# Down projections of the channel mixers by Strassen's method, with the combined weights summed in DRAM

## The chip, the cores and the metric

The kernel runs on one core of a Trainium2 chip. The metric is the device time of one execution in microseconds (us). The time before is 1413.56 us, the median of three runs (1411.99 to 1413.66). A core has five engines, each with its own queue of instructions, worked off in order: PE (matrix products, with PEld loading its weights), DVE (elementwise work), ACT (activations and copies), POOL (a second, slower elementwise engine) and SP (which issues most transfers). Transfers run on 16 DMA engines that all queues share. DRAM is the chip's large memory.

## The reference

A trunk of two layers over 512 tokens of width 1024, in float32. Each layer has a token mixer (layer 0: retention and neighbourhood attention; layer 1: a state space mixer) and a channel mixer, both between norms:

```python
def conv_geglu_ffn(hn, w_up, conv_w, conv_b, w_down):
    u = depthwise_conv_centered(hn @ w_up, conv_w, conv_b)
    gate, val = jnp.split(u, 2, axis=-1)
    return (jax.nn.gelu(gate, approximate=True) * val) @ w_down

def reference(x, ...):
    for layer in range(DEPTH):
        ...
        x = x + rms_norm(m, norm_mix_post[layer])
        f = conv_geglu_ffn(rms_norm(x, norm_ffn_pre[layer]), ffn_w_up[layer], ffn_conv_w[layer],
                           ffn_conv_b[layer], ffn_w_down[layer])
        x = x + rms_norm(f, norm_ffn_post[layer])
    return x
```

The down projection takes a 512 x 2816 activation and a 2816 x 1024 weight to 512 x 1024.

## The kernel before

Every large product is made of three: an operand is split into a high part that PE takes without loss and the low rest (`split`, L92: ACT casts the high part, DVE subtracts to get the low one), and `mm3` (L102) adds high x high, low x high and high x low into one bank of PSUM. A weight tile is 128 x 1024 in float32, 512 KB: SP loads it into one of three buffers `wst` (`wload`, L61), and it is split into `whi` and `wlo`, four buffers each (`wunit`, L69).

The program runs mixer0, the channel mixer of layer 0, mixer1, the channel mixer of layer 1. In mixer0 the values are projected first; then four pairs of heads follow. For each pair `project` (L423 on) makes `rq` and `rk` with rotary: ACT copies the product to `ra`, SP moves its halves crosswise into `rb`, POOL multiplies `rb` by the sines (L444), DVE adds. So POOL has two `rb` for each pair. Ahead of the pairs POOL fills a tile `zero` (L414), and ACT copies it into four tiles (L419).

In the channel mixer (`ffn`, L237) an up projection makes 22 blocks of 128 channels; `tail` (L255) ends each with a convolution, the gate and a split into `hh` and `hl`. The down projection (`down_tm`, L208) then goes by output half n, weight tile and block of 128 tokens t: 22 blocks of channels x 4 blocks of tokens x 2 halves x 3 products, each of 512 columns. When a result (t, n) is complete, `post_half` (L167) takes its sum of squares on ACT and multiplies it by the norm's gains on DVE; `post_norm` adds it to x, `norm` makes the next norm, `turn` transposes it for the next stage.

The order of instructions on each engine is set at build time by a scheduler, which moves an instruction ahead as soon as its inputs are there by the scheduler's own reckoning; on the chip each engine then keeps to that order, and an instruction that waits holds all behind it on its engine. The listings below show that order.

Of the kernel before, what the change touches and what calls it, by code (L numbers as in the profile page):

```python
# [1 line left out]

# [5 lines left out]
F32 = mybir.dt.float32  # L8
# [13 lines left out]
EPS = 1e-6  # L22
FFN = 2816
NF = FFN // P


class Env:


    def __init__(self, ctx, tc):  # L30
        self.tc, self.nc = tc, tc.nc
        nc = self.nc
        pool = lambda name, bufs, **kw: ctx.enter_context(tc.tile_pool(name=name, bufs=bufs, **kw))
# [23 lines left out]
        self.xh = self.res.tile([P, KD, S], R32, name="xh")  # L57
        self.xl = self.res.tile([P, KD, S], R32, name="xl")
        self.late, self.xs, self.turned = [], {}, {}

    def wload(self, src, behind=None):  # L61

# [36 lines left out]
                self.together([m], [b])  # L99
        return first  # L100

    def mm3(self, out, lh, ll, rh, rl, first, last):  # L102
        mm = self.nc.tensor.matmul
        mm(out, lh, rh, start=first, stop=False)  # L104
        mm(out, ll, rh, start=False, stop=False)  # L105
        mm(out, lh, rl, start=False, stop=last)  # L106
# [60 lines left out]
    def post_half(self, st, t, n, ps, g_post, eng=None, m=None):  # L167
# [5 lines left out]
        halves = st.setdefault(t, [])  # L173
        r = self.inv_rms("m", halves[0][0], s) if halves else None
        (eng or nc.vector).tensor_tensor(m, ps, g_post[:, n * 512:(n + 1) * 512], op=ALU.mult)
        halves.append((s, m, r))

    def finish(self, steps, st, done, ahead=0):
        for step in steps.split():
# [13 lines left out]
    def post_norm(self, st, t):  # L193

        nc = self.nc
        (_, m0, _), (_, m1, r) = st[t]
        for h, m in enumerate((m0, m1)):
            xs = self.x[:, t, h * 512:(h + 1) * 512]
            nc.vector.scalar_tensor_tensor(xs, m, r, xs, op0=ALU.mult, op1=ALU.add)

# [33 lines left out]
    E.late += [lambda s=s: E.finish(s, st, done) for s in LATE]  # L234


def ffn(E, w_up, cw, w_down, g_post_row, done, w1=None):  # L237


    nc, tc = E.nc, E.tc  # L240
    with ExitStack() as ctx:
        hp = ctx.enter_context(tc.tile_pool(name="ffn_h", bufs=NF))
        cp = ctx.enter_context(tc.tile_pool(name="ffn_c", bufs=1))
        cwt = cp.tile([P, 2, NF, 4], F32, name="cwt")
        hs = []
# [18 lines left out]
        extra = lambda i=0: [hp.tile([P, S], R32, name=n) for n in ("hh", "hh", "hl", "hl")]  # L264
# [3 lines left out]
        w0 = [[u0, u1], [E.wunit(w_up[0, 1], extra(), st, behind=behind), E.wunit(w_up[1, 1], extra(), behind=behind)]]  # L268
        nc.sync.dma_start(cwt, cw)
        p0 = [[E.mm.tile([P, S], F32, name="mm") for s in range(2)] for f in range(2)]  # L270
        for c in range(2):
            for i in range(4):
                f, s = i // 2, i % 2
                E.proj_fm(p0[f][s], w0[f][s], c * 256, c * 256 + 256)
                if c == 0 and i in (1, 2):
                    E.flush()
        for f in range(2):
            tail(f, *p0[f])
        for f in range(2, NF):
            ps = []  # L280
# [6 lines left out]
            tail(f, *ps)  # L287
        g_post = E.bcast(g_post_row)
        batches = [[(0, u)] for u in (2, 2, 2, 2, 2, 1)] + [[(1, u)] for u in (2, 2, 1, 6)]
        down_tm(E, batches, w_down, lambda k: hs[k], g_post, done, lambda i: extra() if i not in (2, 3) else None)  # L290


def log1p_exp_neg(E, alloc, z):
# [35 lines left out]
def mixer0(E, w0, w_v, w_fm, tabs, dist_d, logit, gn, bias, w_out, g_post_row, done):  # L329
# [4 lines left out]
    with ExitStack() as ctx:  # L334
# [97 lines left out]

        def project(p, o, nm):
            i = ("rk", "rq", "rg", "nq", "nk").index(nm)
            w = E.wunit(w_fm[i, p])
            ps = E.mm.tile([P, S], F32, name="mm")
            E.proj_fm(ps, w)
            if i < 2:
                a = E.tmp.tile([P, S], F32, name="ra", tag="tmp")
                b = E.tmp.tile([P, S], F32, name="rb", tag="tmp")  # L440
                nc.scalar.activation(a, ps, AF.Copy, scale=1.0 if i else 0.125)
                for j in range(4):
                    nc.sync.dma_start(b[32 * j:32 * j + 32], a[32 * (j ^ 1):32 * (j ^ 1) + 32])
                nc.gpsimd.tensor_tensor(b, b, rot[:, 1], op=ALU.mult)  # L444
                nc.vector.tensor_tensor(a, a, rot[:, 0], op=ALU.mult)
# [561 lines left out]
def trunk(tc, x, norms, ab, ssd, ffns, out):  # L1007

    nc = tc.nc
    with ExitStack() as ctx:  # L1010
# [42 lines left out]
        ffn(E, *ffns[1], norms[1, 3], store, w1)  # L1053
        while E.late:
            E.flush()

# [8 lines left out]
def _rows(w, order=None):  # L1065

    k, n = w.shape
    w = w.reshape(k // P, P, n // 512, 512)
    if order is not None:
        w = w[list(order)]  # L1070
    return w.reshape(k // 256, 2, P, n // 512, 512).transpose(3, 0, 2, 1, 4).reshape(n // 512, k // 256, P, 1024)


def _rotary_tables(np):
# [23 lines left out]
def _layouts(np, i):  # L1098
# [34 lines left out]
    for l in range(2):  # L1133
        w = i["ffn_w_up"][l]
        a[f"f{l}_up"] = np.stack([_cols(w[:, s * FFN:(s + 1) * FFN]) for s in range(2)])
        cw = np.concatenate([i["ffn_conv_w"][l], i["ffn_conv_b"][l][None]])
        a[f"f{l}_cw"] = cw.reshape(4, 2, NF, P).transpose(3, 1, 2, 0)
        a[f"f{l}_down"] = _rows(i["ffn_w_down"][l])
    return {n: np.ascontiguousarray(v) for n, v in a.items()}


# [26 lines left out]
```

## Time and profile before

| | |
|---|---|
| median of three runs | 1413.56 us |
| span of the profiled execution, first to last instruction | 1409.7 us |
| PE's granted clock, mean | 0.999 |
| moved by DMA | 166.36 MB, mean 118 GB/s |
| DMA queues | SP's 150.00 MB (34.0% of 16 engines' span), ACT's 15.21 MB (3.8%), none of POOL |

The profile is one execution on the chip. An engine is busy while it executes; "idle before" names what ended its idle time. PE's products overlap, so their single durations add up to more than the time that they take together. The page gives no time of its own for the profiled execution; its span lies 3.9 us under the median of the runs.

### The profile page before, as it was taken

To read this page: it belongs to the slowest core of one execution; us is meant where nothing else is said; L and a number is where in the kernel's file an instruction comes from. 1 tells how busy PE (TensorE), PEld (TensorE's weight loads), DVE (VectorE), ACT (ScalarE), POOL (GpSimd) and SP (SyncE) were. 2 spreads that over 40 slices of the span, in tenths; PEclk is the share of its full clock that TensorE was granted. 3 is DMA by queue.
4 is the path that set the end of the run, shared out by engine and by line. 5 is a ranking of instruction groups with operands and counts; after the bars stand their busy time and mean duration, and the time that the engine had idled before them with its cause. 6 is when DMAs were issued, how large, how long until landed. Compare 5 with 4: busy or idle time off the path is not lost.

```text
span 1409.7 us, 18020 instructions
## 1 busy us (share of the span) xinstructions
PE 1386.0 (98%) x6908; PEld 1144.1 (81%) x6908; DVE 905.1 (64%) x1364; ACT 710.4 (50%) x1203; POOL 62.7 (4%) x66
## 2 busy tenths in 40 slices
PE   7999999999999999999999999999999999999998
PEld 6877787898888888888778787787888888888886
DVE  7378888755566652347878786897786565654232
ACT  5356665544444431324877787477454444442230
POOL 0010110100000000000000110010110000000000
PEclk9999999999999999999999999999999999999999
DMA  8443233222333233333566454273433333232231
GB/s 291 147 141 96 87 97 101 86 86 92 103 91 104 90 90 109 115 113 106 142 185 189 136 182 146 75 212 107 137 120 105 105 90 105 91 105 90 90 105 60
DMA packets 56438, 166.36 MB, mean 118 GB/s; under 512 B 6688, under 2 KB 7456, under 8 KB 56352
## 3 DMA queue, kind: packets, MB, share of 16 engines
q1 hardware_dynamic: 48464, 150.00, 34.0%
q10 hardware_dynamic: 7888, 15.21, 3.8%
q8 instruction: 55, 0.90, 0.3%
q14 instruction: 31, 0.25, 0.1%
HBM read 157.57 MB, written 5.51 MB: 116 GB/s over the span
## 4 chain that ended last, share of the span: by engine, by line
PE 88%; DVE 4%; ACT 3%; DMA 2%; issue 1%; POOL 1%; SPq 0%; DVEq 0%; POOLq 0%; ACTq 0%
PE mm L104 26%; PE mm L106 26%; PE mm L105 26%; PE pi L844 1%; PE st L793 1%; PE py L864 1%; PE pt L161 1%; PE pt L737 1%; PE y L519 1%; ACT pb L823 1%; DMA pb<-pd 0%; ACT junk L141 0%; DMA x<-in_x 0%; DVE wlo L96 0%; ACT whi L95 0%
## 5 line engine op out<-in xcount | busy, mean ns | idle before, releaser
L104 PE MATMUL mm<-xh,whi 128*128 128x512 f32 (+1 forms) x1216 | 463.9, 382 | 0.4 <-ACT xh L95 0.2
L105 PE MATMUL mm<-xh,wlo 128*128 128x512 f32 (+2 forms) x1216 | 462.8, 381 | 1.4 <-DVE wlo L96 1.4
L106 PE MATMUL mm<-xl,whi 128*128 128x512 f32 (+2 forms) x1216 | 463.2, 381 | 0.5 <-DVE xl L96 0.5
L96 DVE TENSOR_TENSOR wlo<-wst,whi 128x1024 fp32r<-128x1024 f32 (+1 forms) x208 | 254.3, 1224 | 137.3 <-ACT whi L95 135.6
L95 ACT CAST whi<-wst 128x1024 fp32r<-128x1024 f32 (+1 forms) x208 | 216.6, 1042 | 147.1 <-PE mm L105 117.7
L104 PEld LDWEIGHTS mm<-xh,whi 128*128 128x128 f32 x1216 | 228.3, 188 | 45.2 <-issue 2.5
L105 PEld LDWEIGHTS mm<-xh,wlo 128*128 128x128 f32 (+1 forms) x1216 | 228.4, 188 | 44.7 <-DVE wlo L96 1.9
L106 PEld LDWEIGHTS mm<-xl,whi 128*128 128x128 f32 (+1 forms) x1216 | 228.1, 188 | 45.0 <-issue 1.3
L251 DVE SCALAR_TENSOR_TENSOR cv<-mm,cwt,cv 128x511 f32<-128x511 f32 x88 | 65.9, 749 | 146.2 <-ACT cv L250 146.2
L250 ACT ACTIVATE cv<-mm,cwt 128x512 f32<-128x512 f32 x88 | 68.7, 780 | 124.5 <-PE mm L106 124.5
L104 PE MATMUL mm<-whi,hh 128*128 128x512 f32 x288 | 112.0, 389 | 0.0
L105 PE MATMUL mm<-whi,hl 128*128 128x512 f32 x288 | 112.0, 389 | 0.0
L106 PE MATMUL mm<-wlo,hh 128*128 128x512 f32 x288 | 112.0, 389 | 0.0
L823 ACT ACTIVATE pb<-pb,tok 128x128 f32<-128x128 f32 x256 | 80.7, 392 | 6.9 <-DMA pb<-pd 5.5
L95 ACT CAST hh<-cv 128x512 fp32r<-128x512 f32 x44 | 27.3, 621 | 103.7 <-DVE cv L259 103.7
L252 DVE SCALAR_TENSOR_TENSOR cv<-mm,cwt,cv 128x511 f32<-128x511 f32 x88 | 66.0, 750 | 3.0
L105 PEld LDWEIGHTS mm<-whi,hl 128*128 128x128 f32 x288 | 54.1, 188 | 11.3
L104 PEld LDWEIGHTS mm<-whi,hh 128*128 128x128 f32 x288 | 54.1, 188 | 11.2
L106 PEld LDWEIGHTS mm<-wlo,hh 128*128 128x128 f32 x288 | 54.1, 188 | 11.2
L757 DVE SCALAR_TENSOR_TENSOR xf<-mm,cwt,xf 128x511 f32<-128x511 f32 (+1 forms) x64 | 47.5, 744 | 6.4 <-ACT xf L754 5.9
L96 DVE TENSOR_TENSOR hl<-cv,hh 128x512 fp32r<-128x512 f32 x44 | 30.5, 693 | 28.9 <-ACT hh L95 28.9
L141 ACT ACTIVATE junk<-mm 128x512 bf16<-128x512 f32 x24 | 14.3, 596 | 67.4 <-PE mm L106 67.3
(267 smaller groups left out, 1871.7 us busy)
## 6 DMA issues: line engine op xcount, KB each, us to landing
wst<-in_f_up SPq DMA_DIRECT2D x88, 512.0 KB
wst<-in_f_down SPq DMA_DIRECT2D x44, 512.0 KB
wst<-in_c_fm SPq DMA_DIRECT2D x40, 512.0 KB
pb<-pd ACTq DMA_DIRECT2D x29, 512.0 KB
wst<-in_ab_fm SPq DMA_DIRECT2D x20, 512.0 KB
gain<-yd SPq DMA_DIRECT2D x32, 256.0 KB
wst<-in_c_out SPq DMA_DIRECT2D x16, 512.0 KB
gain<-in_norms SPq DMA_DIRECT2D x8, 512.0 KB
```

The costliest lines, as they stand in the source:

```text
L95: first = self.nc.scalar.copy(hi, src)
L96: second = self.nc.vector.tensor_tensor(lo, src, hi.bitcast(F32), op=ALU.subtract)
L104: mm(out, lh, rh, start=first, stop=False)
L105: mm(out, ll, rh, start=False, stop=False)
L106: mm(out, lh, rl, start=False, stop=last)
L141: self.nc.scalar.activation(self.junk[:, :w], src, AF.Square, scale=float(n) ** -0.5, accum_out=s)
L161: last = nc.tensor.transpose(pt[:, j], xs[:, j * P:(j + 1) * P], self.ident)
L250: nc.scalar.activation(o, ps, AF.Identity, scale=w(1), bias=w(3))
L251: nc.vector.scalar_tensor_tensor(o[:, 1:], ps[:, :S - 1], w(0), o[:, 1:], op0=ALU.mult, op1=ALU.add)
L252: nc.vector.scalar_tensor_tensor(o[:, :S - 1], ps[:, 1:], w(2), o[:, :S - 1], op0=ALU.mult, op1=ALU.add)
L757: nc.vector.scalar_tensor_tensor(r[:, a], ps[:, b], wc(j), r[:, a], op0=ALU.mult, op1=ALU.add)
L823: nc.scalar.activation(pb[:, dr, c], pb[:, dr, c], AF.Identity, scale=1.0 - 2 * dr, bias=tok[:, 0, c, dr * H + h:dr * H + h + 1])
```

## The change

Each down projection is cut into quarters: the activation by token halves and channel halves, the weight by channel halves and output halves. Strassen's method (in its form with seven products) makes four result quarters from seven products of a 256 x 1408 by a 1408 x 512 quarter, where the plain way has eight. Four of the seven take a sum or difference of weight quarters. These are formed ahead, in DRAM, by DMAs that POOL issues: for each layer 16 copies and 16 adds (`accum_op`), each of a quarter of a quarter, 720,896 bytes, into a DRAM tensor `ts`. Sums of activation quarters are formed by DVE on `H`, which now holds the whole activation unsplit; each product's operand is split in `prepare`. Result quarters share PSUM banks or are added up by DVE (`kept`).

```diff
+HK = NF // 2
+HW = S // 2
+QUARTER = HK * P * S
...
+    def chore(self, n=1):
+
+        for _ in range(min(n, len(self.chores))):
+            self.chores.pop(0)()
...
+def sums(E, w, ts):
...
+    gp = E.nc.gpsimd
+    rows, n = QUARTER // 1024, 4
+    part = lambda a, i, c: a[i].rearrange("(r e) -> r e", e=1024)[c * rows // n:(c + 1) * rows // n]
+    out = []
+    for stage in (((0, w, 0, None), (1, w, 1, None), (2, w, 3, None), (3, w, 2, None)),
+                  ((0, w, 1, ALU.add), (1, w, 3, ALU.add)), ((2, ts, 0, ALU.add),), ((3, ts, 2, ALU.add),)):
+        for i, src, j, op in stage:
+            for c in range(n):
+                kw = dict(accum_op=op, max_dma_last_dim=4096) if op else {}
+                out.append(lambda i=i, src=src, j=j, c=c, kw=kw: gp.dma_start(part(ts, i, c), part(src, j, c), **kw))
+    return out
...
+def down_strassen(E, pool, w, ts, H, first, g_post, done):
...
+        if i == 1:
+            tt(s3, A11, A21, op=ALU.subtract)
+            return s3
+        if i == 2:
+            tt(A21, A22, A21, op=ALU.subtract)
+            stt(A11, A11, -1.0, A21, op0=ALU.mult, op1=ALU.subtract)
+            return A11
+        if i == 6:
+            stt(A11, A12, -1.0, A11, op0=ALU.mult, op1=ALU.subtract)
+            return A11
+        return {3: A12, 4: A21, 5: A22}[i]
...
+    seq = ((w, 0), a), ((ts, 1), bb), ((ts, 2), a), ((w, 2), d), ((ts, 0), a), ((ts, 3), bb), ((w, 3), a)
...
+        for u in range(HK // 2 + 1):
+            ws = weights(src, u)
+            for t in range(2):
+                mms(t, ws, u)
+            if u == 1:
+                nxt = prepare(i + 1)
...
+                nc.vector.tensor_tensor(m, bank[t], m, op=ALU.add)
+                E.post_half(st, tok + t, n, m, g_post, m=m, sign=1.0 - 2 * n)
...
-            nc.vector.tensor_tensor(v, g, v, op=ALU.mult)
-            h = (hp.tile([P, S], R32, name="hh"), hp.tile([P, S], R32, name="hl"))
-            E.split(*h, v)
-            hs.append(h)
...
+            nc.vector.tensor_tensor(H[:, f], g, v, op=ALU.mult)
...
             tail(f, *ps)
+            E.chore(2)
...
         def project(p, o, nm):
             i = ("rk", "rq", "rg", "nq", "nk").index(nm)
+            E.chore(2)
...
+        ts = [E.dram.tile([4, QUARTER], F32, name=f"ts{i}") for i in range(2)]
+        E.chores = sums(E, ffns[0][2], ts[0])
         mixer0(E, w0, *ab, norms[0, 1], then(norms[0, 2]))
-        ffn(E, *ffns[0], norms[0, 3], then(norms[1, 0]))
+        E.chore(len(E.chores))
+        E.chores = sums(E, ffns[1][2], ts[1])
+        ffn(E, *ffns[0], ts[0], norms[0, 3], then(norms[1, 0]))
```

In the program's text the DMAs of layer 0's sums stand two at a time in mixer0's projections, those of layer 1's in layer 0's up projection. Where the scheduler put them shows in POOL's queue. Before, from the start of the program (`r_x` is the first norm, then `zero`, the `rb` of the pairs, and `rs` of the retention's norm):

```order
L134 TENSOR_TENSOR r_x<-ssx,head 128x1 x4
L414 MEMSET zero 128x512
L444 TENSOR_TENSOR rb<-rb,rot 128x512 x3
L533 TENSOR_TENSOR rs<-rs,rg 128x512
L444 TENSOR_TENSOR rb<-rb,rot 128x512 x2
```

Now, the same place, where `ts_222` is layer 0's sums and `ts_223` layer 1's; a row of 16x11264 is a copy, one of 176x1024 an add:

```order
L146 TENSOR_TENSOR r_x<-ssx,head 128x1
L274 DMA ts_222<-in_f_down 16x11264 x11
L274 DMA ts_222<-in_f_down 176x1024 x8
L274 DMA ts_222<-ts_222 176x1024 x8
L274 DMA ts_223<-in_f_down 16x11264 x2
L569 MEMSET zero 128x512
L274 DMA ts_223<-in_f_down 16x11264 x12
L600 TENSOR_TENSOR rb<-rb,rot 128x512
L274 DMA ts_223<-in_f_down 16x11264 x2
L600 TENSOR_TENSOR rb<-rb,rot 128x512
L274 DMA ts_223<-in_f_down 176x1024 x8
L274 DMA ts_223<-ts_223 176x1024 x5
```

All of layer 0's 32 DMAs and two of layer 1's have come to stand ahead of `zero`, and 27 more of layer 1's around the first two `rb` and ahead of the third; the last three stand ahead of the fourth. What these rows wait for, further on in the same queue, around the third and the fourth `rb` (DMASW0 to DMASW7 are eight semaphores that the DMAs of POOL signal in turn, DMAHW those of SP):

```order
L274 DMA ts_223<-ts_223 176x1024 [waits DMASW4_49,DMASW0_49]
L600 TENSOR_TENSOR rb<-rb,rot 128x512 [waits DMAHW6_49,DMAHW5_49,DMAHW7_49,DMAHW4_49,Activation_49]
L274 DMA ts_223<-ts_223 176x1024 [waits DMASW5_49,DMASW1_49]
L274 DMA ts_223<-ts_223 176x1024 [waits DMASW6_49,DMASW2_49]
L274 DMA ts_223<-ts_223 176x1024 [waits DMASW7_49,DMASW3_49]
L600 TENSOR_TENSOR rb<-rb,rot 128x512 [waits DMAHW4_49,DMAHW3_49,DMAHW5_49,DMAHW2_49,DVE_49]
```

The DMAs that stand between them have waits of their own: each for the DMA eight places before it, and these also for the add four places before, whose result they read. The other place is DVE's queue at the start of layer 0's down projection. Before, weight splits (`wlo`) follow each other, with the gain multiplications of results (`mg`) between:

```order
L259 TENSOR_TENSOR cv_4372<-cv_4367,cv_4372 128x512
L96 TENSOR_TENSOR hl<-cv_4372,hh 128x512
L96 TENSOR_TENSOR wlo<-wst,whi 128x1024 x10
L175 TENSOR_TENSOR mg<-mm,gain 128x512 x3
L96 TENSOR_TENSOR wlo<-wst,whi 128x1024
```

Now, at the same place, sums on `H` (L315, L316) and splits of operands (`axl`, `ab1l`) stand between the weight splits:

```order
L108 TENSOR_TENSOR axl<-s_4366,axh 128x1536
L108 TENSOR_TENSOR wlo<-wst,whi 128x1024
L315 TENSOR_TENSOR H<-H 128x11x256
L108 TENSOR_TENSOR wlo<-wx,whi 128x1024
L316 SCALAR_TENSOR_TENSOR H<-H 128x11x256
L108 TENSOR_TENSOR wlo<-wst,whi 128x1024 x2
L108 TENSOR_TENSOR ab1l<-H,ab1h 128x1280
L108 TENSOR_TENSOR wlo<-wst,whi 128x1024
```

What moved is that operations on 2816 columns (11 x 256) now stand in one queue with the weight splits that PE waits for.

More of the change, by code (lines that the diff above doesn't have):

```diff
@@ L1 @@
 from contextlib import ExitStack, nullcontext
+from functools import partial
 import concourse.bass as bass
@@ L100, in split, with mm3 @@
         return first
-    def mm3(self, out, lh, ll, rh, rl, first, last):
-        mm = self.nc.tensor.matmul
+    def mm3(self, out, lh, ll, rh, rl, first, last, more=False):
+        mm = partial(self.nc.tensor.matmul, skip_group_check=True) if more else self.nc.tensor.matmul
         mm(out, lh, rh, start=first, stop=False)
@@ L172, in post_half @@
             m = self.tmp.tile([P, 512], F32, name="mg", tag="tmp")
[L173 to L176, printed above, removed]
+        halves = st.setdefault(t, {})
+        for other, _ in halves.values():
+            halves["r"] = self.inv_rms("m", other, s), None
+            break
+        gs = g_post[:, n * 512:(n + 1) * 512]
+        if sign == 1.0:
+            (eng or nc.vector).tensor_tensor(m, ps, gs, op=ALU.mult)
+        else:
+            nc.vector.scalar_tensor_tensor(m, ps, sign, gs, op0=ALU.mult, op1=ALU.mult)
+        halves[n] = s, m
     def finish(self, steps, st, done, ahead=0):
@@ L195, in post_norm @@
         nc = self.nc
-        (_, m0, _), (_, m1, r) = st[t]
-        for h, m in enumerate((m0, m1)):
+        r, _ = st[t]["r"]
+        for h in range(2):
+            m = st[t][h][1]
             xs = self.x[:, t, h * 512:(h + 1) * 512]
@@ new lines, in down_strassen, with stage, weights, raw @@
+def down_strassen(E, pool, w, ts, H, first, g_post, done):
+    nc, tc = E.nc, E.tc
+    lower, upper = slice(0, HW), slice(HW, S)
+    A11, A21 = H[:, :HK, upper], H[:, :HK, lower]
+    A12, A22 = H[:, HK:, upper], H[:, HK:, lower]
+    k0 = [0]
+    def stage(i, u, cols):
+        st = pool.tile([P, 1024], F32, name="wx") if k0[0] % 4 == 3 else E.wst.tile([P, 1024], F32, name="wst")
+        k0[0] += 1
+        nc.sync.dma_start(st[:, :cols], quarters(*i)[u])
+        return st[:, :cols]
+    def weights(i, u, extra=None):
+        cols = 1024 if u < HK // 2 else 512
+        st = stage(i, u, cols)
+        if extra is None:
+            hi, lo = E.whi.tile([P, 1024], R32, name="whi"), E.wlo.tile([P, 1024], R32, name="wlo")
+        else:
+            hi, lo = extra[:, :1024], extra[:, 1024:]
+        with tc.high_priority(60):
+            E.split(hi[:, :cols], lo[:, :cols], st)
+        return [(hi[:, c:c + 512], lo[:, c:c + 512]) for c in range(0, cols, 512)]
+    a, bb = ([E.mm.tile([P, 512], F32, name="mm") for _ in range(2)] for _ in range(2))
+    s3 = pool.tile([P, HK, HW], F32, name="s3")
+    d = []
+    def raw(i):
+        tt, stt = nc.vector.tensor_tensor, nc.vector.scalar_tensor_tensor
+        if i == 1:
[9 more added lines that the diff above has]
+        return {3: A12, 4: A21, 5: A22}[i]
+    def prepare(i):
+        if i % 2:
+            hi, lo = (E.res.tile([P, HK, HW], R32, name="a" + n, tag=n) for n in ("xh", "xl"))
+        else:
+            hi, lo = (pool.tile([P, HK, HW], R32, name="a" + n, tag=n) for n in ("b1h", "b1l"))
+        src = raw(i)
+        for c in (slice(0, 5), slice(5, HK)):
+            E.split(hi[:, c], lo[:, c], src[:, c])
+        return hi, lo
+    seq = ((w, 0), a), ((ts, 1), bb), ((ts, 2), a), ((w, 2), d), ((ts, 0), a), ((ts, 3), bb), ((w, 3), a)
+    kept = {}
+    st = {}
+    op, nxt = first, None
+    started = []
+    for i, (src, bank) in enumerate(seq):
+        last = i == len(seq) - 1
+        if not bank:
+            bank.extend(E.px.tile([P, 512], F32, name="pd", tag="px") for _ in range(2))
+        more = any(bank is x for x in started)
+        started.append(bank)
+        def mms(t, ws, u):
+            for j, w_ in enumerate(ws):
+                k = 2 * u + j
+                cc = slice(t * P, t * P + P)
+                E.mm3(bank[t], op[0][:, k, cc], op[1][:, k, cc], *w_, not more and k == 0, k == HK - 1, more)
+        if last:
+            ex = {4: pool.tile([P, 2048], R32, name="x1", tag="s3"), 5: pool.tile([P, 2048], R32, name="x2", tag="e2")}
+            ws = [weights(src, u, ex.get(u)) for u in range(HK // 2 + 1)]
+            for t in range(2):
+                for u, x in enumerate(ws):
+                    mms(t, x, u)
+                    if (t, u) == (0, 1):
+                        E.operands()
+                        E.finish("t0", st, done)
+                    if (t, u) == (0, 3):
+                        E.finish("t1", st, done)
+                E.post_half(st, 2 + t, 1, bank[t], g_post, sign=-1.0)
+                E.finish(f"x{2 + t} s{2 + t}", st, done)
+            continue
+        for u in range(HK // 2 + 1):
+            ws = weights(src, u)
+            for t in range(2):
+                mms(t, ws, u)
+            if u == 1:
+                nxt = prepare(i + 1)
+        op = nxt
+        for t in range(2):
+            if i in (0, 1, 2):
+                kept[i, t] = pool.tile([P, 512], F32, name=f"k{i}{t}")
+                nc.scalar.copy(kept[i, t], bank[t])
+            else:
+                j, tok, n = {3: (0, 2, 0), 4: (1, 0, 1), 5: (2, 0, 0)}[i]
+                m = kept[j, t]
+                nc.vector.tensor_tensor(m, bank[t], m, op=ALU.add)
+                E.post_half(st, tok + t, n, m, g_post, m=m, sign=1.0 - 2 * n)
+                if i == 5:
+                    E.finish(f"x{t} s{t}", st, done)
+    E.late += [lambda s=s: E.finish(s, st, done) for s in LATE]
@@ L287, in ffn @@
             tail(f, *ps)
+            E.chore(2)
+            if f == HK + 3:
+                first = [cp.tile([P, HK, HW], R32, name="a" + n, tag=n) for n in ("b1h", "b1l")]
+                for k in range(0, HK, 4):
+                    c = slice(k, min(k + 4, HK))
+                    E.split(first[0][:, c], first[1][:, c], H[:, c, HW:])
         g_post = E.bcast(g_post_row)
-        batches = [[(0, u)] for u in (2, 2, 2, 2, 2, 1)] + [[(1, u)] for u in (2, 2, 1, 6)]
-        down_tm(E, batches, w_down, lambda k: hs[k], g_post, done, lambda i: extra() if i not in (2, 3) else None)
+        down_strassen(E, cp, w_down, ts, H, first, g_post, done)
 def log1p_exp_neg(E, alloc, z):
@@ L1052, in trunk @@
         mixer1(E, *ssd, norms[1, 1], then(norms[1, 2]), ahead)
-        ffn(E, *ffns[1], norms[1, 3], store, w1)
+        ffn(E, *ffns[1], ts[1], norms[1, 3], store, w1)
         while E.late:
```

32 lines of the change are left out of this document (22 added, 10 removed).

## The prediction

> **What bounds the kernel now.** I read the page's engine shares first, then the stage that the change rewrites by a table of windows, then the start of the program, because the change puts new work on POOL and on the DMA engines there.
>
> ```profile
> span 1409.7 us, 18020 instructions
> ...
> PE 1386.0 (98%) x6908; PEld 1144.1 (81%) x6908; DVE 905.1 (64%) x1364; ACT 710.4 (50%) x1203; POOL 62.7 (4%) x66
> 480.00:600.00 120.00, 120.00 (x531) 99.38 (x530) 49.72 (x57) 38.62 (x52) 0.00 (x0) 1.00 0.33 101
> L104 PE MATMUL mm<-whi,hh 128*128 128x512 f32 x288 | 112.0, 389 | 0.0
> ```
>
> The first rows are the span and the share of each engine: PE 98%, nothing else above 64%. The next is the stretch 480 to 600 us, most of it layer 0's down projection, with busy time and count of PE, PEld, DVE, ACT and POOL, then PE's clock, the share of the DMA engines and GB/s: PE is busy throughout, DVE 41%, and the DMA engines a third. So the down projection is bound by PE. The last row is a trap: it gives a product 389 ns, but products overlap. 531 of them passed in 120.00 us, so one costs **0.226 us** of PE, and that is the price I use.
>
> The start of the program looks different:
>
> ```profile
> 8.00:16.00 8.00, 7.00 (x33) 5.79 (x32) 6.32 (x10) 7.87 (x13) 1.65 (x3) 1.00 1.02 412
> 0.00:120.00 120.00, 110.09 (x544) 89.69 (x545) 77.27 (x149) 62.52 (x102) 10.67 (x16) 1.00 0.52 177
> 19.27 0.52 POOL L414 MEMSET zero<- 128x512 f32 x1 [3.33 <-PE pt L161]
> 60.38 1.25 ACT L419 CAST rql<-zero 64x512 fp32r<-64x512 f32 x2
> 77.34 2.01 POOL L444 TENSOR_TENSOR rb<-rb,rot 128x512 f32<-128x512 f32 x1 [57.55 <-DMA rb<-ra]
> 119.66 1.30 POOL L444 TENSOR_TENSOR rb<-rb,rot 128x512 f32<-128x512 f32 x1 [1.04 <-DMA rb<-ra]
> 129.19 0.60 PE L478 MATMUL pt<-head,ra 128*128 128x128 f32 x4
> 78.12 1.79 DVE ra L445
> ```
>
> In the same columns, between 8 and 16 us all DMA engines are full (share 1.02) at 412 GB/s, the fullest stretch that I found; over the first 120 us they carry 177 GB/s, 21.2 MB. POOL is idle there but for a few rows that much hangs on: it fills `zero` at 19.27, which ACT reads at 60.38, and it multiplies `rb`, the rotary's second half, first at 77.34 and for the fourth time at 119.66. What follows from `rb` is on the chain that ended last (the last row is a piece of it), and PE needs the fourth one for the transposes of `ra` at 129.19.
>
> **Part 1, fewer products.** Each layer's down projection is 22 x 4 x 2 x 3 = 528 products of 512 columns; seven quarter products are 7 x 11 x 2 x 3 = 462. Two layers save 132 x 0.226 = **29.8 us**, if DVE and ACT keep up.
>
> **Part 2, more work for DVE.**
>
> ```profile
> L96 DVE TENSOR_TENSOR wlo<-wst,whi 128x1024 fp32r<-128x1024 f32 (+1 forms) x208 | 254.3, 1224 | 137.3 <-ACT whi L95 135.6
> L175 DVE TENSOR_TENSOR mg<-mm,gain x24: 677/682/693, 247.3 to 1404.5; 128x512 f32<-128x512 f32 x24
> L199 DVE SCALAR_TENSOR_TENSOR x<-mg,r_m,x x32: 740/750/754, 249.4 to 1405.9; 128x512 f32<-128x512 f32 x32
> L95 ACT CAST whi<-wst 128x1024 fp32r<-128x1024 f32 (+1 forms) x208 | 216.6, 1042 | 147.1 <-PE mm L105 117.7
> ```
>
> A quarter product lasts 66 x 0.226 = 14.9 us. In it DVE splits 5.5 weight tiles: 5 x 1.22 and a half one at 0.68 (512 columns, as in the second row), 6.8 us. An operation on 2816 columns, at 1.22 us for 1024, takes 3.35 us. In the first product after the opening one DVE also makes two sums and a split for product 2: 6.8 + 3 x 3.35 = 16.9, 2.0 over. In the sixth it makes the last operand's sum and split and four operations of 0.68 on results: 6.8 + 6.7 + 2.7 = 16.2, 1.3 over. In the last one of layer 0 it has four operations on results (2.7), four updates of x (3.0), four normalisations of the same form (3.0) and four splits of turned tokens (2.7): 18.2, 3.3 over; layer 1 has no norm there. Sum: 6.6 + 3.3 = **9.9 us lost**, I take 10. Bounds: nothing, as four split weight tiles are a cover of some 11 us ahead of PE; and all 29.8, as DVE also sits 135.6 us in the program waiting for ACT's cast, and such waits would now fall on a full engine (its sum per layer is about 102 of 104 us). I take the sum from rows. ACT loses nothing by it: casts of 5.5 tiles and one operand at 1.04 us for 1024 columns are 8.6 of 14.9 us. Weight loads rise to 2.88 MB per 14.9 us, 193 GB/s, under half of the 412 above, hidden under the products. The splits that leave the up projection gave PE nothing, since PE is full there; I cost them at nothing.
>
> **Part 3, POOL's queue.** This is the large term. The 64 adding and copying DMAs stand in POOL's queue where the listings show them, not spread over two stages: 16 copies and 16 adds of layer 0 ahead of or around `zero`, nearly all of layer 1's ahead of the fourth `rb`. There are eight completion lanes, so each DMA waits at POOL until the eighth before it has landed, and an add until its source has. Behind a waiting one everything on POOL stands still. Before `zero`, 16 copies and 12 adds must have landed; before the fourth `rb`, 32 copies and 28 adds. Behind `zero` ACT waits in its own order, and behind that the casts of weights that PE needs.
>
> Each of them moves 11 x 128 x 512 x 4 / 4 = 720,896 bytes: 23.1 MB copied, 20.2 MB added. The trace of before has no transfer from DRAM to DRAM and no add, so I bound them by the row of 8 to 16 us. The loads of the first 120 us, 21.2 MB, must pass too, since PE's work up to that point needs them.
> - One pass each: 23.1 + 20.2 + 21.2 = 64.5 MB at 412 GB/s, 157 us from the first us on, so POOL is through at 158. The fourth `rb` slips by 158 - 119.7 = 38; PE's transposes came 9.5 us after it, of which the work between takes about half, so 5 us of that are slack: a stall of 33.
> - Two reads for an add: 84.7 MB, through at 207, a stall of 82.
> - Every pass over DRAM counted, two for a copy, three for an add: 46.1 + 60.6 + 21.2 = 127.9 MB, 310 us, through at 312, a stall of **187**.
>
> I take 187. The nearest row, the 412 GB/s, is one pass over DRAM for each byte (the other end is SBUF), so I count passes. An end further up: adds at half that speed cost 60.6 / 0.412 = 147 more. What POOL needs to issue one is in no row of POOL; the nearest are SP's issues:
>
> ```profile
> L443 SPq DMA_DIRECT2D rb<-ra x32: 507/582/627, 71.4 to 200.4; - x32
> ```
>
> At 0.58 us each, 60 of them are 35 us, which hide under transfers of 3.5 us (two passes of 720,896 bytes at 412 GB/s) or more. I give them nothing, and 35 us if nothing hides them. No later stage holds any of these DMAs but the last four adds.
>
> The rule that a wait stands on the issuing engine can be read in before's rows of the DMA queue's own waits:
>
> ```profile
> SPq L64 <- DVE wlo L96: 917.7, 190, 24.8
> ```
>
> SP stood 917.7 us, 190 times, in front of weight loads until DVE freed a tile. The Trainium skill, DMA: Bandwidth & Descriptors, section Anatomy of one DMA, states it so: DMA engines do not wait on semaphores, the issuing sequencer does; this row agrees. By that rule the stall above stands; if the engines held the wait, the stall would be nothing and the sum 1394. The same page, section Latency and other measured facts, gives 207 to 214 GB/s for copies between HBM tensors; no run here shows it yet. By 214, with adds at half that, copies take 108, adds 189 and loads 51, POOL is through at 349, and the sum would be 1619.
>
> **The sum.** The page's span is 1409.7, 3.9 under the median of 1413.6, which holds the start and end that no instruction fills; no part touches those. 1413.6 - 29.8 + 10 + 187 = **1581 us**. Without part 3 it would be 1394.
>
> **Rivals.**
> - *One pass* (DRAM to DRAM runs as fast as loads): 1394 + 33 = 1427. For it: a copy passes one engine once. Against: those 412 are reached with SBUF at one end. Chance 10%.
> - *Two reads*: copies at the load's speed, adds at half, 1394 + 82 = 1476; with everything between it and the forecast, 24%. The Trainium skill, Collectives: The Full Stack, section The bandwidth ceiling, has the rule: a reduce step is half as fast as a copy, not because of the adding but because two sources are read on one ring. No run here shows it yet; by that rule and loads' speed the result is this rival.
> - *Adds twice as dear* as their passes: 1581 + 147 = 1728; with what lies toward it, 16%.
> - *Faster, the other side*: POOL's queue holds nothing up, and 1394 results. One thing decides: the 60 transfers and the loads must be through by 119.7 + 5 + 20 = 145 us, 64.5 MB at 450 GB/s. The best row here is 412. What speaks for it is only that POOL is 4% busy and that much is early work. Chance 6%.
> - *The change does not do what it says*: DVE so full that the 132 products give nothing, 1581 + 20 = 1601. The count of products is certain, and this lies inside the forecast's case.
>
> **How the numbers follow.** The forecast's case, 1530 to 1640, has 44%; two reads and up to 1530 24%; dear adds 16%; one pass 10%; no hold 6%. The range 1430 to 1700 leaves out the last, most of the one pass end and the far end of the dear adds, near 2 in 10. A measurement here tells 0.2%, 3 us, from no change. Faster is the case without a hold, 6%; between it and one pass lies the little that would be the same, 1%; the rest, 93%, is slower.
>
> **What would show it.** Right: a hole in PE and ACT from about 60 to 80 us on, with ACT waiting for POOL's `zero` until about 150 (before `zero`, 49 MB of passes and 13 MB of loads at 412 GB/s), then `rb` held up, the fourth at about 310; DMA share near 1.0 until then; from there on every stage as long as before, save the two down projections, about 10 us shorter each with DVE over 90% busy. Wrong: DMA share near 1.0 but `zero` on time at 60, or the fourth `rb` before 145, and part 3 falls. If down projections are as long as before, part 2 was too small. Were the DMA share far under 1.0 while POOL waits, it would be not passes but the way of issuing that holds the queue.

## The result, and the profile after

The changed kernel takes **1517.55 us** (median of four runs, 1515.96 to 1521.29); the kernel before took 1412.78 us beside it. The ratio is 1.0748 with a 95% interval of 1.0731 to 1.0765: slower by 105 us. The forecast was 1581, with a range of 1430 to 1700.

The page of the profile after, span, engine shares, slices of the span (38 us each here) and POOL's queue:

```profile
span 1514.4 us, 18049 instructions
...
PE 1372.5 (91%) x6776; PEld 1128.5 (75%) x6776; DVE 983.9 (65%) x1402; ACT 758.2 (50%) x1233; POOL 108.1 (7%) x130
...
PE   3494347999999999999999999999999999999998
...
DMA  9999897332323333256446646426444333332554
...
q0 software_dynamic: 7168, 46.14, 12.3%
```

PE falls from 98% to 91%, and the slices say where: of the first seven, all but the third are empty in part, and in the first six the DMA engines are full (digits 8 and 9). Queue q0 is POOL's; it holds the 64 new transfers, 46.14 MB. The table of windows after, with the columns of the prediction's tables (busy time and count of PE, PEld, DVE, ACT, POOL; PE's granted clock; DMA share; GB/s):

```profile
16.00:60.00 44.00, 12.51 (x57) 9.83 (x57) 9.81 (x17) 5.62 (x10) 8.54 (x15) 0.65 0.99 317
60.00:120.00 60.00, 59.21 (x254) 48.51 (x253) 20.95 (x45) 12.64 (x17) 10.35 (x12) 0.97 1.06 271
120.00:160.00 40.00, 9.25 (x31) 6.80 (x29) 5.05 (x5) 7.91 (x12) 8.19 (x16) 0.65 0.99 308
160.00:200.00 40.00, 22.37 (x115) 18.06 (x115) 23.28 (x55) 18.27 (x36) 9.07 (x10) 0.71 0.90 249
200.00:240.00 40.00, 14.26 (x67) 10.62 (x68) 11.49 (x16) 8.02 (x12) 9.13 (x10) 0.66 0.98 199
240.00:280.00 40.00, 35.57 (x204) 28.52 (x203) 26.30 (x64) 20.66 (x41) 4.70 (x4) 0.96 0.50 123
```

Two holes show in PE's column, one in the row from 16 to 60 us and one from 120 us on, with the DMA engines at 0.9 to 1.06 until 240 and at 0.50 after it. The timeline of POOL after, reduced to the operations that the prediction followed:

```profile
123.93 0.89 POOL L569 MEMSET zero<- 128x512 f32 x1
...
169.10 1.58 POOL L600 TENSOR_TENSOR rb<-rb,rot 128x512 f32<-128x512 f32 x1 [22.04 <-DMA rb<-ra]
...
228.47 1.59 POOL L600 TENSOR_TENSOR rb<-rb,rot 128x512 f32<-128x512 f32 x1
244.25 1.61 POOL L600 TENSOR_TENSOR rb<-rb,rot 128x512 f32<-128x512 f32 x1
```

`zero` has gone from 19.27 to 123.93, the first `rb` from 77.34 to 169.10 and the fourth from 119.66 to 244.25. How much of this remains later is read from one tile that marks the end of every stage, `r_m`, the norm of results (first and last start at the end of each row). Before:

```profile
L134 POOL TENSOR_TENSOR r_m<-v_m,head x16: 537/549/917, 248.8 to 1404.7; 128x1 f32<-128x1 f32 x16
```

After:

```profile
L146 POOL TENSOR_TENSOR r_m<-v_m,head x16: 537/554/926, 377.2 to 1509.0; 128x1 f32<-128x1 f32 x16
```

At the end of mixer0 the program is 377.2 - 248.8 = **128.4 us** late, at its own end 104.3. So the start costs 128.4, the rest of the program gains 24.1, and nothing else is needed to account for the 105 us. The chain of waits after, its DMA pieces up to the fourth `rb` (start, duration):

```profile
13.04 43.52 DMA wst<-in_ab_v
...
68.17 20.04 DMA wst<-in_ab_fm
90.65 9.31 DMA wst<-in_ab_fm
101.61 15.86 DMA nvd<-nv
119.61 15.38 DMA nvt<-nvd
135.00 31.88 DMA nvt<-nvd
...
188.75 0.87 POOL ts L274
...
244.25 1.61 POOL rb L600
```

This is not what the prediction described. Up to 167 us the chain goes through **SP's own loads**: a weight tile that took 43.52 us, and `nvt`, a transfer of 128 KB, that took 15 to 32. Only behind them does it go through POOL's queue (`ts`) to the fourth `rb`. The experiments are built on that difference.

### The profile page after: what moved, and what is told of

Same layout as the page of the kernel before. It is cut to its first block, busy times and chain, and to the rows that moved or that the text cites. A ratio compares the mean times of both kernels' runs of the same rounds, so it can differ in the third digit from the quotient of the medians.

```text
span 1514.4 us, 18049 instructions
## 1 busy us (share of the span) xinstructions
PE 1372.5 (91%) x6776; PEld 1128.5 (75%) x6776; DVE 983.9 (65%) x1402; ACT 758.2 (50%) x1233; POOL 108.1 (7%) x130
## 3 DMA queue, kind: packets, MB, share of 16 engines
q0 software_dynamic: 7168, 46.14, 12.3%
## 4 chain that ended last, share of the span: by engine, by line
PE 74%; DMA 10%; issue 5%; DVE 5%; ACT 4%; POOL 2%; SPq 0%; DVEq 0%; POOLq 0%; ACTq 0%
PE mm L116 22%; PE mm L117 21%; PE mm L118 21%; DMA nvt<-nvd 3%; DMA wst<-in_ab_v 3%; DMA wst<-in_ab_fm 2%; PE pi L1000 1%; PE st L949 1%; DMA nvd<-nv 1%; PE py L1020 1%; POOL ts L274 1%; ACT whi L107 1%; DVE wlo L108 1%; PE pd L117 1%; PE pd L116 1%
## 5 line engine op out<-in xcount | busy, mean ns | idle before, releaser
L108 DVE TENSOR_TENSOR wlo<-wst,whi 128x1024 fp32r<-128x1024 f32 (+1 forms) x232 | 278.7, 1205 | 66.3 <-ACT whi L107 65.2
L107 ACT CAST whi<-wst 128x1024 fp32r<-128x1024 f32 (+1 forms) x232 | 239.3, 1032 | 153.2 <-PE mm L117 71.4
L116 PE MATMUL mm<-whi,xh 128*128 128x512 f32 x104 | 42.3, 411 | 37.4 <-ACT xh L107 36.6
L117 PE MATMUL mm<-whi,ab1l 128*128 128x512 f32 x164 | 64.7, 394 | 0.0
L116 PE MATMUL mm<-whi,ab1h 128*128 128x512 f32 x164 | 64.3, 392 | 0.0
L118 PE MATMUL mm<-wlo,ab1h 128*128 128x512 f32 x164 | 63.8, 389 | 0.0
L116 PEld LDWEIGHTS mm<-whi,xh 128*128 128x128 f32 x104 | 20.4, 197 | 42.5 <-ACT xh L107 37.5
L405 ACT ACTIVATE cv<-cv 128x512 f32<-128x512 f32 x44 | 27.8, 633 | 42.3 <-DVE cv L400 42.2
L117 PE MATMUL mm<-whi,xl 128*128 128x512 f32 x104 | 42.5, 408 | 0.0
L116 PE MATMUL mm<-whi,yh 128*128 128x512 f32 x104 | 40.8, 394 | 1.6 <-DVE xf L913 1.6
```

Of the source, the lines that this page charges most:

```text
L107: first = self.nc.scalar.copy(hi, src)
L108: second = self.nc.vector.tensor_tensor(lo, src, hi.bitcast(F32), op=ALU.subtract)
```

## The experiments

Two theories. The *queue* theory is the prediction's: POOL's adding DMAs hold up POOL's own arithmetic, and all else follows. The *contention* theory: the transfers take the DMA engines from SP's loads, whoever waits on POOL.

### Both halves of the change, each without the other

`no_sums` leaves POOL's DMAs out; the four combined weight quarters are replaced by plain ones of the same size, so the products are those of other operands.

```diff
-    seq = ((w, 0), a), ((ts, 1), bb), ((ts, 2), a), ((w, 2), d), ((ts, 0), a), ((ts, 3), bb), ((w, 3), a)
+    seq = ((w, 0), a), ((w, 1), bb), ((w, 2), a), ((w, 2), d), ((w, 0), a), ((w, 3), bb), ((w, 3), a)
...
-        E.chores = sums(E, ffns[0][2], ts[0])
...
-        E.chores = sums(E, ffns[1][2], ts[1])
```

> No DMA of POOL is left: the products that took summed weight quarters read plain quarters, so the output is not the reference's, and the work of PE, DVE, ACT and SP is that of the change. Markers in the changed kernel's trace (POOL's norm steps) put the gain of the two Strassen stages at some 25 us. If the DMAs are the whole loss: 1412.8 - 25 = 1388, between 1383 (all of the 29.8 of PE's saving) and 1393 (my sum with 10 lost on DVE). Rival, that the stages themselves lose something at the start of the program, too (other order, other tiles): above 1400.

`sums_alone` is the kernel before with the 64 DMAs at the same places of its text; nothing reads their result.

```diff
+        flat = lambda w: w.rearrange("n u p c -> (n u p c)").rearrange("(i e) -> i e", i=4)
+        E.chores = sums(E, flat(ffns[0][2]), ts[0])
...
+        E.chores = sums(E, flat(ffns[1][2]), ts[1])
```

> The kernel before with the 64 DMAs of POOL added where the change has them in the text, and nothing reading their result. If the loss is theirs alone: 1412.8 + 129 = 1542, with POOL's fourth rb near 244 us. If the loss needs the rest of the change, clearly less, under 1500.

Measured: `no_sums` 1390.87 us, ratio 0.9847 [0.9832, 0.9862] to the kernel before; `sums_alone` 1540.52 (one run). The two add up: the products give 21.3 of 1412.1 us, the DMAs cost some 128, and 1390.87 + 128 is the changed kernel's time within 2 us. The whole loss is in the DMAs.

### POOL's arithmetic out of the queue

`arith_on_dve` leaves the DMAs where they are and moves what waited behind them.

```diff
-        nc.gpsimd.memset(zero, 0.0)
+        nc.vector.memset(zero, 0.0)
...
-            nc.gpsimd.tensor_tensor(b, b, rot[:, 1], op=ALU.mult)
+            nc.vector.tensor_tensor(b, b, rot[:, 1], op=ALU.mult)
...
-            nc.gpsimd.tensor_tensor(rs, rs, o["rg"], op=ALU.mult)
+            nc.vector.tensor_tensor(rs, rs, o["rg"], op=ALU.mult)
```

> The change, with POOL's arithmetic in mixer0 (zero, rb, rs) made by DVE, so that nothing of mixer0 stands behind POOL's DMAs; the DMAs run as before. Theory of the prediction (POOL's queue holds the program): 1388 plus a few us for DVE's added work, 1390 to 1410. Rival (the 64 DMAs fill the DMA engines, and SP's loads and the small moves nvd, nvt, rb come late): the first rb came 92 us late in the changed kernel before POOL's later adds could hold it, so some 92 of 129 us stay, 1475 to 1485.

Measured: 1503.02 us (one run). The queue theory as the whole cause expected 1390 to 1410 and **fell**; only 14.5 us went. The chain of this kernel shows why:

```profile
13.18 44.79 DMA wst<-in_ab_v
...
122.38 49.44 DMA nvt<-nvd
177.47 11.13 DMA rb<-ra
```

The weight tile takes as long as in the changed kernel (44.79 us against 43.52), and the 128 KB of `nvt` take 49.44, with `zero`, `rb` and `rs` gone from POOL's queue. The contention theory gave 1475 to 1485 and was short by 18 us: more of the loss stayed than it had reckoned from the first `rb`.

### Who takes the DMA engines

The view of the DMA queues of the kernel after, first for 18 to 38 us (copies), then for 60 to 118 us (adds): packets, MB, and the time that they took as a share of 16 engines. q0 is POOL's, q1 is SP's.

```profile
q0 software_dynamic: 278, 6.26, 90.5%
q1 hardware_dynamic: 279, 0.71, 11.1%
...
q0 software_dynamic: 2157, 8.11, 70.1%
q1 hardware_dynamic: 2483, 7.71, 35.5%
```

In the first stretch the two queues got the same number of packets through, 278 and 279. But a packet of POOL's is 6.26 MB / 278 = 22.5 KB and one of SP's 2.5 KB, so SP got a tenth of the time: 0.71 MB in 20 us is 36 GB/s, where SP moved 4.67 MB (234 GB/s) in the same 20 us of the kernel before. This agrees with a rule of the Trainium skill, DMA: Bandwidth & Descriptors, section Queues, rings and completion order: an engine takes turns between its queues packet by packet. The copies' rows are of 11264 elements (45 KB); the adds are cut into rows of 4096 bytes already, and in the second stretch SP has a third of the time.

`rows_4k` cuts the copies like the adds.

```diff
-                kw = dict(accum_op=op, max_dma_last_dim=4096) if op else {}
+                kw = dict(accum_op=op, max_dma_last_dim=4096) if op else dict(max_dma_last_dim=4096)
```

> The change with its copies in rows of 4 KB (as its adds have them) in place of 45 KB. In the changed kernel's trace POOL's DMAs and SP's loads had the same number of packets while copies ran (278 and 279 between 18 and 38 us), but 6.26 against 0.71 MB. Theory that DMA engines take turns by packet, so that large packets starve SP: SP's first weights come some 25 us sooner and the values' loads nvt take far less than their 50 us; but POOL's queue still stands between, with the same bytes: fourth rb at 225 to 245 us, time 1495 to 1520. Theory of bytes alone: nothing moves, 1515 to 1522, and SP's share of the bytes stays as it was.

`rows_and_dve` has this and the edit of `arith_on_dve`.

> Both edits: copies in rows of 4 KB, and POOL's arithmetic of mixer0 on DVE. If turns by packet and POOL's order are the two causes, either of which keeps the time up while the other stays: 1420 to 1450, far under the 1503 with the arithmetic alone moved. If the bytes alone saturate the DMA engines: 1490 to 1505.

Measured: `rows_4k` 1514.2, `rows_and_dve` 1445.1 us (one run each). In `rows_4k`, 18 to 56 us, the loads have their turn:

```profile
q0 software_dynamic: 2391, 8.96, 60.4%
q1 hardware_dynamic: 2055, 6.15, 41.8%
```

SP gets 6.15 MB in 38 us, 162 GB/s; in the changed kernel it got 1.50 MB in these 38 us, 39 GB/s. Yet the time is all but that of the changed kernel (3 us, in one run), because `zero` still waits in POOL's queue, until 135.14 us in this kernel, and its `rb`:

```profile
135.14 0.55 POOL L569 MEMSET zero<- 128x512 f32 x1
162.15 1.27 POOL L600 TENSOR_TENSOR rb<-rb,rot 128x512 f32<-128x512 f32 x1
...
243.23 1.61 POOL L600 TENSOR_TENSOR rb<-rb,rot 128x512 f32<-128x512 f32 x1
```

The fourth `rb` is at 243.23, against 244.25. The chain of waits of this kernel over its first 250 us no longer names `wst` or `nvt`. By line it reads:

```profile
by line: issue 71.8%; POOL ts L274 15.8%; DMA x<-in_x 4.0%; POOL rb L600 2.3%; ACT junk L153 0.9%; DVE ra L602 0.5%; ACT rq L584 0.5%; ACT rk L561 0.5%; POOL rs L689 0.5%; SPq L1170 0.3%; ACT whi L107 0.3%; ACT rq L582 0.3%; POOL r_x L146 0
```

From 17 us to the fourth `rb` it goes almost wholly through POOL's DMAs (`ts`) and the pauses between them, which the view calls "issue". So the path that was hidden behind SP's loads in the changed kernel is now the one that ends last. There are **two causes, and each alone keeps most of the time up**: one edit gives 3 us, the other 14.5, both 72. That is why neither theory could win by a single edit. What is left, 1445.1 against 1390.9, 54 us, stays with both edits made, so neither POOL's arithmetic in the queue nor the long rows account for it. Windows of `rows_and_dve`:

```profile
16.00:60.00 44.00, 39.80 (x173) 32.39 (x173) 27.49 (x57) 13.54 (x22) 7.62 (x13) 0.92 1.02 392
60.00:120.00 60.00, 38.62 (x171) 31.66 (x169) 9.22 (x9) 13.66 (x19) 10.37 (x12) 0.84 1.02 236
```

The first hole is gone (PE 39.80 of 44.00; 12.51 in the changed kernel), but the DMA engines are as full as ever and PE still waits from 60 us on.

### Copies without adds

`copies_alone` leaves the 32 adds out, so the combined quarters are bare copies; queue and rows are as in the change.

```diff
-                  ((0, w, 1, ALU.add), (1, w, 3, ALU.add)), ((2, ts, 0, ALU.add),), ((3, ts, 2, ALU.add),)):
+                  ):
```

> The change without its 32 adds, so that the output is not the reference's; the 32 copies stay at the start of the program. 23.1 MB at the 346 GB/s that copies reached take 67 us, in which SP gets about a tenth: its weights stand still from 16 to some 80 us, against a first weight then needed at about 25. Turns by packet: a loss of 45 to 65 against 1390, 1435 to 1455. If adds made the loss: under 1410.

Measured: 1456.74 us (one run), just over the range that turns by packet gave. Copies cost 66 us over `no_sums`, the adds of the same bytes 61 on top.

### Holding the sums to another stage

`held_to_up` ties each pair of DMAs to the end of a block of its own layer's up projection by a dependency, so that the scheduler can't hoist it.

```diff
-    def chore(self, n=1):
+    def chore(self, n=1, after=None):
...
-            self.chores.pop(0)()
+            m = self.chores.pop(0)()
+            if after:
+                self.together([m], [after])
...
-            tail(f, *ps)
-            E.chore(2)
+            E.chore(2, tail(f, *ps))
```

(`tail` returns its multiplication into `H`, `project` issues no DMAs, and `E.chores = sums(...)` stands ahead of each layer's `ffn`.)

> The change, with each layer's 32 DMAs held by a dependency to its own up projection, two behind each block of channels from the third on; the start of the program has none. Nothing on POOL waits there, and the DMA share there was a third. If neither order nor contention matters there: 1388. If the DMAs starve the weight loads of the up projections, too: above 1400, up to 1500; the trace then shows waits for in_f_up.

Measured: **1390.48 us, ratio 0.9846 [0.9829, 0.9862]**, as fast as `no_sums`: here the sums cost nothing that can be measured. Page and windows of this kernel:

```profile
PE 1358.1 (98%) x6776; PEld 1118.3 (81%) x6776; DVE 985.6 (71%) x1402; ACT 758.7 (55%) x1233; POOL 107.5 (8%) x130
...
300.00:500.00 200.00, 200.00 (x884) 165.62 (x883) 114.03 (x134) 76.88 (x94) 21.97 (x32) 1.00 0.76 210
```

In the up projection PE is busy throughout, though the share of the DMA engines rises to 0.76, from 0.30 in that stage of the kernel before. Its queues, for copies (314 to 400 us) and adds (412 to 482 us):

```profile
q0 software_dynamic: 512, 11.54, 35.8%
q1 hardware_dynamic: 2304, 8.39, 32.1%
...
q0 software_dynamic: 2387, 8.96, 70.8%
q1 hardware_dynamic: 1910, 6.91, 26.7%
```

While the adds ran, both queues together took 97.5% of the engines, as much as at the start of the changed kernel. But SP still moved 6.91 MB in 70 us, 99 GB/s, and the whole stage had moved 93 GB/s before: there the loads got what they need. What lets them was not taken apart.

`spread` uses the same dependency, but leaves the DMAs where the text has them: layer 0's in mixer0's projections, layer 1's in layer 0's up projection.

```diff
+            self.together([m], [after or self.last])
...
-        mm(out, lh, rl, start=False, stop=last)
+        self.last = mm(out, lh, rl, start=False, stop=last)
```

> The change, with each DMA held by a dependency to the place where its text stands: layer 0's two at a time behind mixer0's projections, layer 1's in layer 0's up projection. If the hoisting to the start is the fault, not the amount of work: 1390 to 1400. If copies starve SP's loads in mixer0 as well: 1400 to 1430, with waits for in_ab_fm and for the halves of rb.

Measured: 1418.49 us, ratio 1.0048 [1.0032, 1.0063]. So undoing the hoisting gives back 99 us (1517.55 - 1418.49), but half the bytes, put into mixer0 as written, still cost 28 us against `held_to_up`. Is that rows, queue or bytes? `spread_4k` adds the edit of `rows_4k`, `spread_4k_dve` that of `arith_on_dve` too, and `held_dve` is `held_to_up` with the latter alone, as a control.

> The kernel spread (1418.5 us, 28 over the version held to the up projections) with its copies cut into rows of 4096 bytes as well, so that their packets take fair turns with those of the loads. If large rows are what costs the 27 us that mixer0 lost in spread, this one comes to 1390 to 1402, and the last rb to within 10 us of before's 202.59. If mixer0 has no room for the bytes of the sums, or POOL's queue costs it the time, 1410 to 1425, with the last rb near 225 to 232.

> The kernel spread_4k (1415.4 us) with the fill of zero and the products of rb and rs in mixer0 moved from POOL to DVE, so that a DMA that waits at POOL holds up no arithmetic. If POOL's queue is what mixer0 lost its 25 us to, this comes to 1390 to 1401 (with what the arithmetic costs DVE, read from held_dve). If the bytes alone cost it, 1408 to 1418, and between these both have a share.

> The version held to the up projections (1390.5 us) with the same three operations on DVE: what the move costs by itself. Twelve products of 512 columns at about 0.7 us in stretches where DVE is 70 to 87% busy: 1390 to 1397.

Measured: `spread_4k` 1415.38, ratio 1.0027 [1.0014, 1.0039]; `spread_4k_dve` 1415.18, ratio 1.0012 [0.9998, 1.0026]; `held_dve` **1387.92, ratio 0.9827 [0.9806, 0.9847]**, the lowest of all and 2 us under the range expected, though its interval overlaps that of `held_to_up`. Large rows cost some 3 us here, which the intervals hardly tell apart, and the queue no more than that (the edit by itself gave 2.6 in `held_dve`, and nothing in `spread_4k_dve`): what is left in mixer0, by elimination, is **the transfers themselves**. Two rows of waits say the same directly. `spread_4k_dve` and `held_dve` both have the arithmetic on DVE, and DVE's idle time before `rb` is, first in `spread_4k_dve`, then in `held_dve` (us, times):

```profile
DMA rb<-ra: 29.4, 5
...
DMA rb<-ra: 0.3, 1
```

Behind one of these waits PE stands for 19.4 us in the first kernel, and for 0.3 in the second. The chain of `spread_4k_dve`:

```profile
67.32 9.37 DMA nvt<-nvd
76.71 14.42 DMA nvt<-nvd
91.15 6.68 DMA rb<-ra
...
182.16 6.17 DMA rb<-ra
```

The same kind of piece in the chain of the kernel before:

```profile
68.20 5.05 DMA nvt<-nvd
73.29 3.74 DMA rb<-ra
```

Mixer0 has short round trips through DMA, and beside the sums each takes some two to three times as long, although the DMA engines are not full there (a share of 0.72 to 0.87 between 60 and 240 us; 0.29 to 0.42 before). With half of the bytes the stage is 274.1 - 248.8 = 25 us late at its end (`r_m` starts there at 274.1).

## Why the prediction came out as it did

**Part 1, the products: right.** 6776 products instead of 6908. One reading beside it was loose: in the row of shares that the prediction shows, PEld stands at 81%, so it is not true that nothing else is above 64%. PEld is PE's own loading of weights, and no term was built on it.

**Parts 1 and 2, net 19.9 forecast: near, but not for the reason given.** `no_sums` gained 21.3, and the changed kernel 24.1 after mixer0. DVE's crowding cost PE nothing. The windows of the kernel after, in layer 0's down projection:

```profile
608.00:712.00 104.00, 104.00 (x459) 85.84 (x458) 75.72 (x70) 55.78 (x64) 0.00 (x0) 1.00 0.47 150
```

PE is full and DVE is at 75.72 / 104 = 73%, not above 90% as forecast. Single bursts do fill DVE: in `held_to_up` it is busy for 19.92 us between 520 and 540, and PE for all 20. My sums for single products charged such bursts to PE; the bound that the prediction names, split tiles waiting ahead of PE, fits what was measured, but was not tried by itself. The 8 us that are missing from 29.8 lie elsewhere in `held_to_up`. PE's busy sum fell by 1386.0 - 1358.1 = 27.9, and its idle time rose from 23.7 to 30.0, by 6.3. 2.3 of that are at the join of layer 0's channel mixer and mixer1. That window in `held_to_up`:

```profile
600.00:700.00 100.00, 97.08 (x516) 78.84 (x515) 84.11 (x140) 64.10 (x113) 6.81 (x8) 1.00 0.50 153
```

And before:

```profile
600.00:700.00 100.00, 99.40 (x530) 82.75 (x530) 66.35 (x114) 51.11 (x87) 4.39 (x8) 1.00 0.36 115
```

The last tokens' norms come in pairs at the end of Strassen's last product, where before they came one by one. Whether this is the reason was not tried. Most of the rest lies in mixer1 and its join with layer 1's channel mixer: from 600 to 1100 us, the window above included, PE is idle for 10.9 us in `held_to_up` and for 5.3 before, 5.6 of the 6.3. Its cause stays open.

**Part 3, place and sign: right; size: wrong.** The DMAs do come ahead of `zero` and `rb`, and the fourth `rb` sets the end of the stall. It was forecast at 312 and came at 244.25; the stall was 128.4, not 187. So the time, 1517.55, lies in the case that had 24%, and not in the forecast's own, 1530 to 1640, which had 44%. The step that failed is "I count passes": every pass over DRAM charged at the loads' 412 GB/s, two for a copy and three for an add. The queues of the kernel after, from 0 to 244 us:

```profile
q0 software_dynamic: 6901, 45.18, 74.0%
q1 hardware_dynamic: 7680, 21.71, 24.6%
```

The byte count was right (the loads: 21.71 MB against 21.2), and the engines were full, 98.6% with both. The rates were not. Copies: 6.26 MB in 90.5% of 20 us is 346 GB/s (375 in `held_to_up`), nearly the loads' rate. Adds: 8.11 MB in 70.1% of 58 us is 199 GB/s (181 in `held_to_up`). So 23.1 MB of copies took 67 us instead of 112, 22.1 MB of adds 111 instead of 161 (three passes at 412; the prediction had counted 20.2 MB of them, 147 us), and the loads 60 instead of 51: 238 of the 244 us. That is the *two reads* rival in its rates: a copy costs one pass, an add two. Its time, 1476, was still 42 too low: it had the fourth `rb` at 207, 37 too early (412 for copies and loads, and half of it for adds, were all somewhat high), and it gave PE 5 us of slack behind `rb`, where the stall, 128.4, was longer than the delay of `rb`, 124.6. Of the pages' figures, the Trainium skill's half rate for a reduce step (Collectives: The Full Stack, section The bandwidth ceiling) agrees with 181 to 199 against 346 to 375; the two source reads that it gives as the reason were not isolated here. Its 207 to 214 GB/s for copies between HBM tensors (DMA: Bandwidth & Descriptors, section Latency and other measured facts) is stated there for tiles of 128 rows of 16 KiB from the queues of SP and ACT, and does not hold for these copies from POOL's queue, in rows of 45 KB.

**Part 3, mechanism: half right.** I let POOL's queue carry the whole stall. The bytes of SP's loads were in the sum, but nothing was charged for their coming late. `arith_on_dve` refutes that: with nothing of mixer0 behind POOL's DMAs it still takes 1503. The stall has three parts on top of each other: POOL's queue, the unequal turns of long rows, and the traffic itself. That a sum of bytes over a rate came as near as it did is in part luck: it holds wherever the DMA engines are full up to the fourth `rb`, whether `rb` waits for POOL's queue or for SP's loads. Two signs of the part of SP's loads stand in the profile after. `zero` came at 123.93, before the 150 forecast, while PE's first hole, forecast from 60 to 80 us on, began at 26.6 and was over at 58.2: there PE waited for a cast of ACT, and ACT for a load `wst`, 32.1 us by the table of waits, not for POOL. The sign that I had named for it (DMA share near 1.0 with `zero` late) could not tell the three apart, because all of them show it. The chain of waits does: it names `wst` and `nvt`, not POOL, up to 167 us.

**The other rivals.** *One pass* (1427) fits the copies and not the adds. *Adds twice as dear* and *no hold* fell with the rates and the stall. *The change does not do what it says* fell with `no_sums`.

## What to carry to other kernels

A transfer that nobody waits for still costs what it takes from those that somebody waits for. Give such work, with a dependency, to a stage that is bound by an engine and whose own loads take little of the DMA engines (a share of 0.30 here), and don't leave its place to a scheduler that sees only that its inputs are ready: the same 64 transfers cost 128 us at the start of this program and nothing beside the up projection. When two causes overlap, removing either shows almost nothing (3 and 14.5 us here); try both together before dropping one.

## What the runs showed of the hardware that was not expected

- Two queues that both have work share the DMA engines by packets, not by bytes: 278 against 279 packets, 22.5 KB against 2.5 KB each. (In `held_to_up`, where POOL's DMAs come two at a time, the counts are 512 and 2304.) Cutting the long rows to 4096 bytes brought SP from 39 to 162 GB/s between 18 and 56 us, while POOL's queue went from 10.43 to 8.96 MB; both together moved 15.1 MB, 398 GB/s.
- Copies from DRAM to DRAM ran at 346 to 375 GB/s per full share, adds at 181 to 199.
- PE's granted clock was 0.65 to 0.71 in the windows in which it was busy for a quarter to a little over half of the time (16 to 60 and 120 to 240 us after), and 0.97 to 1.00 in those that it filled. In the chain after, products behind the first hole take 0.43 us each until 63.5 us and 0.23 from 63.9 on. PE's busy sum is 1372.5 us, 14.4 more than in `held_to_up` for the same 6776 products; by this estimate slower products are some 14 of the 127 us between the two kernels.
